# Four banks for an up-projection, two loads taken by turns, and a convolution that is not paused, in a hybrid encoder layer

## The chip, the cores and the metric

The kernel runs on one NeuronCore of a Trainium2 chip. The metric is the device time of one execution in microseconds (us); a time for a kernel is the median of its runs. A profile is one more execution, recorded by the hardware profiler, and its times count from the first instruction of its span. The engines are PE (TensorE, matmuls; PEld is its weight loads), DVE (VectorE), ACT (ScalarE), POOL (GpSimd) and SP (SyncE, which issues most DMAs).

## What is computed

One encoder layer, run on two requests that share all weights: a prompt of 512 rows and a sample of 1024 rows, 1024 wide, all in fp32.

```python
def _trunk(x, ...):                       # called for the prompt and for the sample
    h = _rmsnorm(x, norm_attn_g)
    z = h @ w_in                          # 1024 x 1792: q, k, v, ca, cb
    a_out = _window_attn(q, k, v, ...)    # 8 heads, 2 kv heads, |q-k| <= 128, bias, sink
    c = ca * sigmoid(cb)
    c = _dwconv(c, conv_dw_w, conv_dw_b)  # 31 taps, 512 channels
    c = silu(_layernorm(c, ...))
    x = x + concat([a_out, c]) @ w_out
    h = _rmsnorm(x, norm_ffn_g)
    u = _dwconv(h @ w_up, ffn_dw_w, ffn_dw_b)            # 3 taps, 5632 channels
    x = x + (silu(u[..., :2816]) * u[..., 2816:]) @ w_down
    return _rmsnorm(x, norm_final_g)
```

## The kernel before, in words

**Numbers.** Every fp32 matmul operand is split into two fp32r parts, `hi` (a cast on ACT) and `lo` (a subtraction on POOL or DVE). A product is three matmuls per 128 rows of contraction: hi·hi, hi·lo, lo·hi. A weight block of 128 columns is split by `split` (L158): one ACT instruction (L161) and one POOL instruction (L162).

**Tiling.** Activations are held transposed, 128 channels on the partitions by 512 tokens: one piece for the prompt (`nt` 0), two for the sample (`nt` 1 and 2). A product of a weight block with one piece (`proj`, L304) is 8 x 3 = 24 matmuls of 128x512 into one PSUM bank.

**Banks.** Up to the sample's MLP the eight PSUM banks have names: three `a`, two `u`, two `b`, one `c`. The table `use` (L123, updated at L853, L902, L1005, L1026, L1052) says which letters a job may take, and `Slots.tile` (L82) takes the first free one in the order in which they were given back. In the prompt's MLP the jobs are: `up` (the products), `gate` (on `b`), `attn` and `turn` (on `a`), `norm` (on `a` and `u`, then `a`), `conv` (on `c`).

**Start.** SP issues the loads in program order. First come the prompt's transposed input in eight chunks and the first weight block in five pieces. Then `load_rows(0)` (L209) loads the prompt's four blocks of 128 rows, 512 KB each, and `load_xT(1)` (L199) the sample's first piece, transposed, in four chunks of 512 KB. The rows feed `row_scale(0)` (L492): a sum of squares of each block (ACT L247 and DVE L249 by turns), a reciprocal root on POOL (L145, L146), four ACT spreads (L255), four PE transposes (L258) and an ACT copy (L499); the result scales the products of the prompt when they are taken from their banks (`evac`, L388). The transposed chunks feed `raw_h1` (L471): one ACT (L474) and one DVE instruction (L475) per 128 channels. `beside` (L515) makes the products of the first two weight blocks with one piece: 48 matmuls at L519, for the prompt, then the sample's pieces.

**Middle.** The prompt's projection, convolution (`conv_items`) and attention run beside the projection of the sample; then the prompt's output projection. The sample's convolution (`late_items`, L366) is a queue `late` of steps: one DVE instruction per tap (L345), every second one with a tap on ACT and POOL (L336, L337) while there are some left to hand over.

**The prompt's MLP.** Twenty-two pieces (L1044). `ffn_step(k)` (L996) makes two products, gate half and value half, with weights that were split a piece earlier. `up_half` (L942) takes a product from its bank with one ACT (L958) and two DVE instructions (L954), the last readers of the bank; `gate` (L972) puts the halves together in a `b` bank (ACT L974, DVE L975 and L976) and stores the result. Beside it run the sample's attention (`side`) and `late`. Both are advanced by `tick` (L286), which `proj` calls three times and `up_mm` once per product: each call adds `pace["late"]` to a credit, and queue steps are issued while there is credit; a tap costs 0.13 + 512/960 = 0.663 of it. `pace["late"]` is `CD` = 0.65 from piece `LK` on and 0 before.

**Then** come the sample's output projection and its MLP on wide banks, a seven-product (Strassen-like) scheme, up-projection and down-projection.

**Order.** The program text gives priorities. A planner orders each engine's instructions by a simulated timeline and these priorities, so an engine may run a later piece of text first when the earlier one isn't ready in the simulation. On the chip each engine keeps the planned order. From L1345 on the order of PE is that of the text.

Of the kernel before, what the change touches and what calls it, by code (L numbers as in the profile page):

```python
# [59 lines left out]
SA, N2, SA2 = 4, 99, 4  # L60
KL, WN = 16, 7
LN = 3
LK = 1
AHEAD = (1, 1, 1, 2, 2)
XQ, H2, LATE2 = (1, 5), 2, (4,)
SUM_AT = (4, 6, 8, 10, 12, 14, 16, 18)
# [41 lines left out]
def tile_hybrid_encoder(ctx: ExitStack, tc: tile.TileContext, xs, rel_bias, norm_attn_g, w_in,  # L108
# [11 lines left out]
    sb = Slots(lambda tag: sml if tag[0] == "s" else big,  # L120
               dict(q=(15, 4096), c=(4, 4352), h=(61, 2048), d=(2, 2304), s=(33, 64)))
    banks = Slots(lambda tag: ps[two_of[tag]], dict(a=(3, 2048), u=(2, 2048), b=(2, 2048), c=(1, 2048)))
    use = dict(step="aub", turn="aub", conv="c", attn="au", norm="b", out="b", up="u", down="b")  # L123

    def sm(n):
        return sb.tile([n])
# [1 line left out]
    def bank(job):  # L128
        return banks.tile([NT], among=use[job])
# [18 lines left out]
    def load_x(G, tt):  # L148
        x = sb.tile([D])
        nc.sync.dma_start(x[:], G["x"][tt * P:(tt + 1) * P, :])  # L150
        return x
# [23 lines left out]
    def want_raw(i):  # L175
        if i < nch and i not in raws and i not in ws:
            raws[i] = chunk_raw(laid["w_in"], order[i][2] // P)

    def want_w(i):
        if i < nch and i not in ws:  # L180
            want_raw(i)
            ws[i] = split(raws.pop(i))
# [16 lines left out]
    def load_xT(nt):  # L199
        n = 1 if nt == 0 else 2  # L200
        for k in range(0, KC, n):
            x = sb.tile([n, NT])
            nc.sync.dma_start(x[:], xT[nt][k:k + n].rearrange("k p t -> p k t"))
            for m in range(n):
                xq[nt, k + m] = (x, m)
            x = None
            yield

    def load_rows(nt):  # L209
        G, t0 = (GR[0], 0) if nt == 0 else (GR[1], 4 * (nt - 1))  # L210
        for tt in range(4):
            xq[nt, "row", tt] = load_x(G, t0 + tt)

    def drawn(items):
        for _ in items:
            pass
# [12 lines left out]
    for i, n in enumerate(AHEAD):  # L229
        load_first(i, nc.sync)  # L230
        for _ in range(n):
            next(x_of_prompt)
    drawn(x_of_prompt)
    load_rows(0)
    drawn(load_xT(1))
    for _ in range(NW // 4):
        pt = bank("step")
        for i in range(4):
# [232 lines left out]
    def raw_h1(nt, kc):  # L471
        t, m = xq.pop((nt, kc))
        x, hi, lo = t[:, m, :], sb.tile([NT], F32R), sb.tile([NT], F32R)
        nc.scalar.activation(hi[:], x, AF.Identity, scale=gA[:, kc:kc + 1])  # L474
        nc.vector.scalar_tensor_tensor(lo[:], x, gA[:, kc:kc + 1], hi[:].bitcast(F32), op0=ALU.mult, op1=ALU.subtract)  # L475
        h1.setdefault(nt, []).append((hi, lo))
# [15 lines left out]
    def row_scale(nt):  # L492
        ss, rs = sm(4), sm(4)
        for tt in range(4):
            square_sum(xq.pop((nt, "row", tt)), ss[:, tt:tt + 1], tt)
        rstd_of(ss[:], D, rs[:])
        pt = spread(rs, "turn")
        rbs[nt] = sb.tile([NT])
        nc.scalar.copy(rbs[nt][:], pt[:])  # L499
# [7 lines left out]
    def landed(i, nt, pp):  # L507
        kind, c, col = order[i]
        evac(kind, c, nt, pp[:])
        if kind == "ca" and nt != 1:  # L510
            g = min(nt, 1)
            (convs, late)[g].append((conv_items, late_items)[g](c, cpads.pop((g, c))))
        tick()

    def beside(nt, kc, first=False):  # L515
        hi, lo = h1[nt][kc]
        for L, R in ((0, hi), (0, lo), (1, hi)):
            for c in range(2):
                nc.tensor.matmul(pps[nt, c][:], ws[c][L][:, kc, :], R[:], start=(kc == 0 and L == 0 and R is hi),  # L519
                                 stop=(kc == KC - 1 and L == 1))  # L520
# [16 lines left out]
    ends = cvw[:, :(CK - 1) * 4].rearrange("p (s h c) -> p h s c", h=2, c=4)  # L537
    nc.gpsimd.tensor_tensor(csum[:, :CK // 2 * 4].rearrange("p (s c) -> p s c", c=4), ends[:, 0], ends[:, 1], op=ALU.add)
    nc.gpsimd.tensor_copy(csum[:, CK // 2 * 4:CK // 2 * 4 + 4], cvw[:, (CK - 1) * 4:CK * 4])
    load_rows(1)  # L540
    for kc in range(KC):
        raw_h1(1, kc)

    def constants():
        nc.vector.tensor_scalar_mul(vecs[:, 20:28], vecs[:, 20:28], 0.5)
        nc.vector.tensor_scalar_mul(vecs[:, 50:72], vecs[:, 50:72], 0.5)
        halves = fw[:, :132].rearrange("p (t f) -> p t f", t=3)[:, :, 22:44]
        nc.vector.tensor_scalar_mul(halves, halves, 0.5)
        nc.vector.tensor_scalar_mul(nsink[:], sinkb[:], -1.0)
# [28 lines left out]
    for nt in range(3):  # L578
        if nt:
            pps.update({(nt, c): bank("step") for c in range(2)})  # L580
            for kc in range(KC):
                beside(nt, kc)
        if nt == 1:
            for kc in range(KC):
                raw_h1(2, kc)
            want_w(2)
            row_scale(1)
            want_raw(3)
            load_rows(2)
            constants()  # L590
        if nt == 2:
            row_scale(2)
            want_w(3)
        for i in range(2):
            landed(i, nt, pps.pop((nt, i)))
# [238 lines left out]
    def double_keys():  # L834
        for kv in range(NKV):
            for L in range(2):
                nc.gpsimd.tensor_copy(kt[1, kv][L][HD:P, :], kt[1, kv][L][0:HD, :].bitcast(F32))
                yield
# [28 lines left out]
    def prompt_out():  # L867
        for n in range(2):
            for kc in range(KC):
                if (kc, n) not in wor:  # L870
                    load_wo(kc, n)
            yield 0.0
            for kc in range(KC):
                split_wo(kc, n, kc % 2 < DW)
                if kc % 2 == 1:
                    yield 0.0
            for i in range(4):
                if n == 0 and i == 3:
                    for kc in range(WOP):
                        load_wo(kc, 1)  # L880
                while i not in ready:
                    yield 0.0
                yield from out_half(i, n)
            wo.clear()
        bias.clear()
        load_bias(1)
        yield from make_h2(0, 0)
# [19 lines left out]
    out = deque([prompt_out()])  # L907
    n, doubling = 0, double_keys()
# [135 lines left out]
    for k in range(NJ):  # L1044
        at[0] = k
        if k == LK:
            pace.update(late=CD)
# [34 lines left out]
    A, rows = {}, {}  # L1082
# [631 lines left out]
    u, e, o11, o12 = (acc.pop(n) for n in ("u", "e", "o11", "o12"))  # L1714
# [108 lines left out]
```

## Time and profile before

| | |
|---|---|
| time, median of 3 runs | 1501.19 us (1499.17 to 1506.18) |
| the profiled execution | 1498.89 us |
| its span, first to last instruction | 1497.1 us |
| PE, DVE, ACT, POOL busy | 1473.5, 1119.2, 803.7, 770.7 us |
| mean DMA rate | 152 GB/s |
| mean granted TensorE clock | 0.999 |

A busy time is the union of an engine's instructions. Matmuls overlap: a row gives 389 ns for one, and 112 of them run in 25 us. Idle time of PE is therefore read from the gaps, not from the rows' sums. A wait is put down to the instruction whose semaphore came last; that name can be of a neighbour that ended at the same moment.

### The profile page before, as it was taken

Reading aid. Unit: us, or ns where it says so; the run is one execution under the profiler, and the core shown is the slowest. Engines: PE = TensorE matmul, PEld = TensorE weight load, DVE = VectorE, ACT = ScalarE, POOL = GpSimd, SP = SyncE. Lnnn points to the kernel's source line nnn. Section 1 sums busy time; section 2 is a strip of 40 time slices with the busy share of each in tenths; the row PEclk is TensorE's granted clock in tenths of the full one; section 3 lists DMA queues with packets and bytes.
Section 4 is the critical chain, followed back from the end, with each engine's and each line's share of the span. In section 5 each row is a group of like instructions: output and inputs, shape, how many; then the busy total and the mean of one; then the engine's idle time right before and its main releaser. Section 6 shows DMA issues by size and latency. Waiting matters only on the chain.

```text
span 1497.1 us, 19881 instructions
## 1 busy us (share of the span) xinstructions
PE 1473.5 (98%) x6736; PEld 1211.2 (81%) x6736; DVE 1119.2 (75%) x1512; ACT 803.7 (54%) x1421; POOL 770.7 (51%) x687
## 2 busy tenths in 40 slices
PE   9999999999999999999999999999999999999998
PEld 7888778877888888878878888888888888888886
DVE  7877935649898998575768888888887856578774
ACT  7424455567777676653465544544454543343355
POOL 3455353347878776432336666565555242135546
PEclk9999999999999999999999999999999999999999
DMA  9554241743344454663214333334342495356644
GB/s 368 187 153 144 91 113 36 242 159 127 127 139 136 130 166 141 209 216 116 79 57 137 131 125 129 125 121 129 132 134 68 155 315 187 116 194 213 222 167 162
DMA packets 124626, 228.19 MB, mean 152 GB/s; under 512 B 20420, under 2 KB 45764, under 8 KB 124397
## 3 DMA queue, kind: packets, MB, share of 16 engines
q1 hardware_dynamic: 124092, 226.37, 46.1%
q8 instruction: 53, 0.87, 0.3%
q10 hardware_dynamic: 432, 0.56, 0.1%
q14 instruction: 49, 0.39, 0.1%
HBM read 166.83 MB, written 61.10 MB: 152 GB/s over the span
## 4 chain that ended last, share of the span: by engine, by line
PE 74%; DVE 5%; DMA 3%; POOL 3%; issue 2%; ACT 2%; SPq 0%; POOLq 0%; DVEq 0%; ACTq 0%
PE w L1187 8%; PE w L1189 8%; PE w L1188 8%; PE w L1519 7%; PE w L1520 7%; PE w L1521 7%; PE u L308 5%; PE u L309 5%; PE u L310 5%; PE b L310 2%; PE b L308 2%; PE b L309 2%; PE a L685 1%; PE a L643 1%; DVE c L345 1%
## 5 line engine op out<-in xcount | busy, mean ns | idle before, releaser
L162 POOL TENSOR_TENSOR q<-q,q 128x1024 fp32r<-128x1024 f32 x66 | 158.8, 2407 | 77.2 <-ACT q L161 51.1
L1067 POOL TENSOR_TENSOR q<-q,q 128x512 fp32r<-128x512 f32 x81 | 116.5, 1447 | 126.7 <-ACT q L1173 126.7
L1067 DVE TENSOR_TENSOR h<-h,h 128x512 fp32r<-128x512 f32 (+1 forms) x152 | 129.5, 881 | 55.4 <-ACT h L1075 21.8
L1521 PE MATMUL w<-h,h 128*128 128x512 f32 x432 | 168.1, 389 | 0.0
L1519 PE MATMUL w<-h,h 128*128 128x512 f32 x432 | 168.1, 389 | 0.0
L1520 PE MATMUL w<-h,h 128*128 128x512 f32 x412 | 160.3, 389 | 0.0
L308 PE MATMUL u<-h,q 128*128 128x512 f32 x384 | 150.8, 393 | 2.5 <-DVE s L658 2.1
L310 PE MATMUL u<-h,q 128*128 128x512 f32 x384 | 150.6, 392 | 0.0
L309 PE MATMUL u<-h,q 128*128 128x512 f32 x384 | 150.3, 391 | 0.0
L1187 PE MATMUL w<-h,q 128*128 128x512 f32 x368 | 143.8, 391 | 0.5 <-ACT w L1260 0.4
L1189 PE MATMUL w<-h,q 128*128 128x512 f32 x368 | 143.7, 391 | 0.0
L1188 PE MATMUL w<-h,q 128*128 128x512 f32 x347 | 135.5, 390 | 0.0
L1067 POOL TENSOR_TENSOR h<-h,h 128x512 fp32r<-128x512 f32 (+1 forms) x38 | 51.8, 1364 | 142.8 <-ACT h L1502 123.9
L1075 ACT CAST h<-h 128x512 fp32r<-128x512 f32 x116 | 69.2, 620 | 103.4 <-DVE h L1067 27.9
L161 ACT CAST q<-q 128x1024 fp32r<-128x1024 f32 x66 | 69.2, 1049 | 53.9 <-PE u L309 24.0
L345 DVE SCALAR_TENSOR_TENSOR c<-d,cvw,c 128x512 f32<-128x512 f32 x128 | 95.9, 749 | 1.5
L337 POOL TENSOR_TENSOR h<-h,h 128x512 f32<-128x512 f32 x62 | 80.8, 1304 | 28.8 <-ACT h L336 26.9
L1521 PEld LDWEIGHTS w<-h,h 128*128 128x128 f32 x432 | 81.1, 188 | 16.9
L1519 PEld LDWEIGHTS w<-h,h 128*128 128x128 f32 x432 | 81.1, 188 | 16.9
L1067 POOL TENSOR_TENSOR c<-q,c 128x512 fp32r<-128x512 f32 x46 | 72.0, 1572 | 42.0 <-ACT c L1173 42.0
L1520 PEld LDWEIGHTS w<-h,h 128*128 128x128 f32 x412 | 77.3, 188 | 15.9
L308 PEld LDWEIGHTS u<-h,q 128*128 128x128 f32 x384 | 72.1, 188 | 16.9 <-ACT h L336 2.3
(474 smaller groups left out, 4019.4 us busy)
## 6 DMA issues: line engine op xcount, KB each, us to landing
q<-in_laid_w_up SPq DMA_DIRECT2D x88, 512.0 KB, 3.9
ga<-q SPq DMA_DIRECT2D x65, 256.0 KB, 2.2
h<-gap SPq DMA_DIRECT2D x57, 256.0 KB, 3.5
h<-ga SPq DMA_DIRECT2D x57, 256.0 KB, 3.4
h<-in_w_down SPq DMA_DIRECT2D x52, 256.0 KB, 3.5
q<-in_laid_w_in SPq DMA_DIRECT2D x22, 512.0 KB, 4.1
gap<-h SPq DMA_DIRECT2D x44, 256.0 KB, 3.1
q<-in_x_sample SPq DMA_DIRECT2D x15, 512.0 KB, 7.2
```

What stands on the lines that cost most here:

```text
L162: (nc.vector if dve else nc.gpsimd).tensor_tensor(lo[:], raw[:], hi[:].bitcast(F32), op=ALU.subtract)
L308: nc.tensor.matmul(out, whi[:, kc, :], hi[:], start=(kc == 0), stop=False)
L309: nc.tensor.matmul(out, whi[:, kc, :], lo[:], start=False, stop=False)
L310: nc.tensor.matmul(out, wlo[:, kc, :], hi[:], start=False, stop=(kc == KC - 1))
L345: nc.vector.scalar_tensor_tensor(acc[:], src(t), w(t), acc[:], op0=ALU.mult, op1=ALU.add)
L1067: (eng or nc.vector).tensor_tensor(out, a, b, op=ALU.subtract)
L1187: nc.tensor.matmul(out, whi[:, s], hi[:], start=(start and c == 0), stop=False, **go)
L1188: nc.tensor.matmul(out, whi[:, s], lo[:], start=False, stop=False, **go)
L1189: nc.tensor.matmul(out, wlo[:, s], hi[:], start=False, stop=(stop and c == 3), **go)
L1519: nc.tensor.matmul(out, sh[:, c], th[:], start=(p == 0 and not seeded), stop=False, **go)
L1520: nc.tensor.matmul(out, sh[:, c], tl[:], start=False, stop=False, **go)
L1521: nc.tensor.matmul(out, sl[:, c], th[:], start=False, stop=(p == NPAIR - 1), **go)
```

## The change

`use["up"]` becomes `"ub"`: the products of the prompt's MLP may take the two `u` banks and the two `b` banks, which `gate` also takes. `LK` becomes 0: `late` goes on through piece 0. `load_rows` becomes a generator; at the start SP issues by turns one block of rows and one chunk of the sample's transposed input. The other two calls of `load_rows` draw all four blocks at once, as before.

```diff
-LK = 1
+ROWS = (1, 1, 1, 1)
+LK = 0
...
-    use = dict(step="aub", turn="aub", conv="c", attn="au", norm="b", out="b", up="u", down="b")
+    use = dict(step="aub", turn="aub", conv="c", attn="au", norm="b", out="b", up="ub", down="b")
...
         for tt in range(4):
             xq[nt, "row", tt] = load_x(G, t0 + tt)
+            yield
...
-    load_rows(0)
-    drawn(load_xT(1))
+    rows, x_of_sample = load_rows(0), load_xT(1)
+    for n in ROWS:
+        for _ in range(n):
+            next(rows)
+        next(x_of_sample)
+    drawn(rows)
+    drawn(x_of_sample)
...
-    load_rows(1)
+    drawn(load_rows(1))
...
-            load_rows(2)
+            drawn(load_rows(2))
```

## The prediction

> **What bounds the kernel now.** I read the page's busy times first, then PE's time in stretches that follow the stages, then PE's waits, and then the order of time at the two places that these point to.
>
> ```profile
> span 1497.1 us, 19881 instructions
> PE 1473.5 (98%) x6736; PEld 1211.2 (81%) x6736; DVE 1119.2 (75%) x1512; ACT 803.7 (54%) x1421; POOL 770.7 (51%) x687
> ...
> PE 74%; DVE 5%; DMA 3%; POOL 3%; issue 2%; ACT 2%; SPq 0%; POOLq 0%; DVEq 0%; ACTq 0%
> ```
>
> PE works 1473.5 of 1497.1 us: it stands still for 23.6 us in all. The change issues the same matmuls, so it can only move these 23.6 us. The next view has PE alone by stretches (length, PE busy, instructions, clock, DMA).
>
> ```profile
> core 0: us, PE busy (x), PEclk, DMA share, GB/s
> 0.00:25.00 25.00, 21.53 (x89) 1.00 0.95 345
> 25.00:150.00 125.00, 125.00 (x566) 1.00 0.58 186
> 150.00:338.00 188.00, 181.80 (x883) 1.00 0.42 127
> 338.00:364.00 26.00, 22.75 (x104) 1.00 0.39 134
> 364.00:636.00 272.00, 271.56 (x1294) 1.00 0.47 149
> 1300.00:1325.00 25.00, 25.00 (x112) 1.00 0.49 151
> ```
>
> Idle: 3.5 us in the first 25, none to 150, 6.2 to 338, 3.3 in the first pieces of the prompt's MLP, 0.4 in the rest of it. The last row gives the pace: 25 / 112 = 0.223 us per matmul where all are 128x512; I take 0.23 in the busier early stages. The waits name what ended the idle times (waiter, releaser: us in total, times, longest):
>
> ```profile
> PE u L308 <- DVE s L658: 2.1, 1, 2.1
> PE a L519 <- ACT h L474: 1.8, 1, 1.8
> PE b L308 <- DVE h L457: 1.3, 1, 1.3
> PE a L643 <- DVE s L647: 1.1, 1, 1.1
> PE a L685 <- DVE s L647: 1.0, 2, 0.5
> PE u L308 <- DVE h L954: 0.4, 1, 0.4
> ```
>
> The two longest are the places of the change. No wait comes back piece after piece.
>
> **Rows by turns.** The start, in order of time (start, length, engine, line; [idle before it <- what ended it]):
>
> ```profile
> 13.69 1.06 ACT L247 ACTIVATE h<-q 128x1024 bf16<-128x1024 f32 x1 [0.51 <-DMA q<-in_x_prompt]
> 16.22 1.06 ACT L247 ACTIVATE h<-q 128x1024 bf16<-128x1024 f32 x1 [1.38 <-DMA q<-in_x_prompt]
> 17.36 0.39 PE L519 MATMUL b<-h,h 128*128 128x512 f32 x1
> 17.44 1.23 DVE L249 CUSTOM_DVE_ANT_0 h<-q 128x1024 bf16<-128x1024 f32 x1 [1.21 <-DMA q<-in_x_prompt]
> 18.73 1.34 ACT L474 ACTIVATE h<-q,vecs 128x512 fp32r<-128x512 f32 x2 [1.35 <-DMA q<-in_laid_xsT]
> 19.50 2.45 PE L519 MATMUL a<-h,h 128*128 128x512 f32 x8 [1.75 <-ACT h L474]
> 21.79 0.38 PE L258 MATMUL b<-ident,h 128*128 128x128 f32 x2
> 25.05 0.56 ACT L499 COPY h<-b 128x512 f32<-128x512 f32 x1
> 26.29 0.68 DVE L395 TENSOR_TENSOR h<-u,h 128x512 f32<-128x512 f32 x1
> 42.22 0.39 PE L308 MATMUL b<-h,q 128*128 128x512 f32 x1
> ```
>
> ACT and DVE were waiting for each transfer, so these starts are its landings: the first block of rows at 13.7, the third at 16.2, the fourth at 17.4, the sample's first chunk at 18.7. A 512 KB transfer lands every 1.25 us. The prompt's last matmul starts at 17.36, PE could go on at 17.59, and it begins the sample's at 19.50: 1.91 us lost, for the chunk that is fifth in the row. By turns the chunk is second and lands near 13.7 + 1.25 = 14.95. ACT has ended its sum of squares at 14.75, so the first `hi` is there at 15.7 and its `lo`, at 0.75 us, near 16.5: PE does not wait. Two 128-channel steps of `beside` need 12 x 0.23 = 2.7 us and a chunk now comes every 2.5; the fourth lands at 22.5 as before and is wanted at 17.6 + 3 x 2.7 = 25.7, with 1.5 us for ACT and DVE. So -1.9 us. The price: the fourth block of rows lands at about 21.2, 3.8 us later, and so do the sums, POOL's root, L258 (21.8 to 25.6), L499 (28.9) and the first L395 (30.1). Who needs them: the banks that L395 frees, first asked for after the products that start at 42.2; 12 us of cover. The SP queue holds the same eight issues, so nothing behind them moves. Is the 1.9 kept? From 25 to 150 PE never waits, so it is carried to 150. At 154 to 158 PE waits for DVE (1.1 and 1.3 us above) with DVE nearly full:
>
> ```profile
> 125.00:150.00 25.00, 25.00 (x123) 20.92 (x122) 23.27 (x48) 11.95 (x30) 13.27 (x16) 1.00 0.44 130
> 77.68 0.70 DVE L409 TENSOR_TENSOR u<-u,h 128x512 f32<-128x512 f32 x1 [5.37 <-PE u L310]
> ```
>
> DVE had 5.4 us of idle behind PE at 77.7, so DVE's own work moves up with PE there. I take -1.9; bounds -2.0 and +3.8 (L258's delay, if PE has to wait for it in its order).
>
> **Four banks.** The first pieces of the prompt's MLP:
>
> ```profile
> 343.72 2.42 POOL L162 TENSOR_TENSOR q<-q,q 128x1024 fp32r<-128x1024 f32 x1
> 345.04 3.92 DVE L345 SCALAR_TENSOR_TENSOR c<-c,csum,c 128x512 f32<-128x512 f32 x5
> 348.85 2.42 POOL L162 TENSOR_TENSOR q<-q,q 128x1024 fp32r<-128x1024 f32 x1
> 351.19 1.45 ACT L958 ACTIVATE h<-u,vecs,fw 128x512 f32<-128x512 f32 x2
> 352.98 0.74 DVE L954 SCALAR_TENSOR_TENSOR h<-u,fw,h 128x511 f32<-128x511 f32 x1
> 353.12 0.66 PE L685 MATMUL a<-ident,h 128*128 128x128 f32 x4 [0.54 <-DVE s L647]
> 354.30 1.40 DVE L954 SCALAR_TENSOR_TENSOR h<-u,fw,h 128x511 f32<-128x511 f32 x2
> 355.84 0.47 PE L308 MATMUL u<-h,q 128*128 128x512 f32 x1 [2.07 <-DVE s L658]
> ```
>
> PE has ended the transposes of 353.12 at 353.78 and the third product starts at 355.84. It needs the bank of the first, whose taps are L954 at 352.98 and the second of the pair at 354.30, ended at 355.70; the named L658 is a reciprocal that it does not read. Its weights were split by 346.1 (L162 at 343.72). Before the MLP eight transposes go over `u`, `u`, `c`, `b`, `b`, so the free order is u, u, b, b: the third product now takes a `b` bank, free since the transposes. That takes away 2.07 us, and the 0.4 us of the other product that waits for L954: -2.5. What is late next: the fourth product takes the first's bank, at 353.78 + 24 x 0.23 = 359.3; the taps end at 355.7 and its weights at 351.3 (L162 at 348.85): covered. The 0.5 us waits at L685 are on `a` banks and stay. Bounds: -2.8 (start to start instead of idle) and 0 (the wait goes over to the next product).
>
> **Gates on the same banks.** By the free order every third piece from piece 4 on begins with a product on a bank that a gate two pieces back gave up; six times.
>
> ```profile
> 386.91 0.69 DVE L976 TENSOR_TENSOR h<-b,h 128x512 f32<-128x512 f32 x1
> 393.62 0.47 PE L308 MATMUL u<-h,q 128*128 128x512 f32 x1
> ```
>
> Piece 2's gate ends at 387.6 and piece 4's first product starts at 393.6: 6.0 us of cover, so 0.
>
> **Convolution not paused.** Piece 0 gets 8 ticks x 0.65 = 5.2 of credit, 5.2 / 0.663 = 8 taps: on DVE 8 x 0.749 = 6.0 us, and 4 taps handed over, on POOL 4 x 1.304 = 5.2 us.
>
> ```profile
> L345 DVE SCALAR_TENSOR_TENSOR c<-d,cvw,c 128x512 f32<-128x512 f32 x128 | 95.9, 749 | 1.5
> L337 POOL TENSOR_TENSOR h<-h,h 128x512 f32<-128x512 f32 x62 | 80.8, 1304 | 28.8 <-ACT h L336 26.9
> ```
>
> The planner had already put taps there (five at 345.04), so part of the 8 is no new work in piece 0. In POOL's queue they stand before the splits for the fourth product, done 8.0 us ahead of need: covered. On DVE they stand before the first product's taps: at worst 355.7 + 6.0 = 361.7 against 359.3, +2.4 us. Best -1.0, if the two L685 waits go with the new order. I take 0, as DVE's own idle and the taps already there are nearest.
>
> **Sum.** 1498.9 - 1.9 - 2.5 = 1494.5 for a profiled execution. That one lay 2.3 below the median of the runs, so 1496.8: 1497.
>
> **Rivals.** *Given back*: DVE, not PE, paces 150 to 175 and the first pieces (the 23.27 of 25 above), so PE comes earlier and waits longer. Against it is DVE's idle at 77.7. It gives 1500 to 1501. [...] The trace shows the bank as the cause of the one, so I give this a quarter.
>
> *The row scale stalls PE (slower)*: L258 stood behind 8 matmuls of the sample. If the plan leaves it so, PE reaches it at 17.6 + 8 x 0.23 = 19.4 and waits to 25.6; PE is 3.8 late instead of 1.9 early: 1501.2 + 3.8 - 2.5 = 1502.5. It decides when L258 stands before the 35th of the 48 matmuls ((25.6 - 17.6) / 0.23). Against it: the planner knows the new loads. [...]
>
> *Gates hold the banks (slower still)*: if gates end over 6.0 us later, six products wait. With gates 8 us later it is 6 x 2 = 12: 1509. It needs a DVE order that no row shows.
>
> *More than the sum*: the new plan also closes half of the 6.2 us between 150 and 338 and the two L685 waits: 1497 - 4 = 1493.
>
> **Chances.** Forecast 0.52, given back 0.25, row scale 0.08, gates 0.05, more 0.10. Range: 1491 takes in the lower bounds (-2.0, -2.8, -1.0) and most of the last case; 1504 the row scale; only gates and tails are left out. This kernel's measurement tells 0.5%, 7.5 us, from no change: under 1493.7 lies part of the last case and scatter, 0.09; over 1508.7 the gates, 0.05; the rest, 0.86, between.
>
> **What would show it.** Right: no wait of L519 for L474 near 17 to 20, and the sample's products begin by 17.8; no wait of an up product for L954 or L658; PE's idle sum near 19 us. Wrong: L258 after an idle PE; products that wait for L976; L345 ahead of L954 with PE idle at 359; or the waits near 155 grown by 1.9.

## The result, and the profile after

The changed kernel takes 1497.95 us (median of 17 runs, 1496.36 to 1501.16), the kernel before 1501.75 in the 17 runs beside them (1499.01 to 1506.18). The ratio is 0.9974, 95% interval 0.9967 to 0.9982: 2.7 to 5.0 us faster, inside the 0.5% that I called no change. The forecast was 1497.0 with the range 1491 to 1504. The sum behind it did not come out so well, and that the two times lie so near each other is luck: two gains were put too small, one term was nought and is a loss, and a fourth effect was not in the sum.

The page of the changed kernel, its busy times and the shares of the chain:

```profile
span 1496.9 us, 19874 instructions
PE 1475.7 (99%) x6736; PEld 1215.0 (81%) x6736; DVE 1120.4 (75%) x1512; ACT 801.8 (54%) x1421; POOL 771.9 (52%) x687
...
PE 87%; DVE 4%; DMA 3%; POOL 3%; ACT 2%; issue 1%; SPq 0%; POOLq 0%; DVEq 0%; ACTq 0%
```

The profiled span is 0.2 us shorter than before's 1497.1, though the medians are 3.8 apart. PE's idle time fell from 23.6 to 1496.9 - 1475.7 = 21.2, that is -2.4; but PE's busy time rose from 1473.5 to 1475.7, +2.2, with the same 6736 matmuls. They ran slower. The same stretches as in the prediction (length, PE busy, instructions, clock, DMA), and one more:

```profile
core 0: us, PE busy (x), PEclk, DMA share, GB/s
0.00:25.00 25.00, 23.22 (x96) 1.00 0.95 346
25.00:150.00 125.00, 124.33 (x565) 1.00 0.59 190
150.00:338.00 188.00, 179.59 (x858) 0.98 0.40 122
338.00:364.00 26.00, 25.92 (x119) 0.95 0.43 142
364.00:636.00 272.00, 272.00 (x1299) 1.00 0.47 151
...
150.00:165.00 15.00, 12.51 (x50) 0.77 0.20 69
```

Length less busy gives the idle time of each, against before: 1.8 (3.5), 0.7 (0), 8.4 (6.2), 0.1 (3.3), 0 (0.4). The start and the prompt's MLP gained 1.7 + 3.2 + 0.4 = 5.3 us; the stretch in between gave back 0.7 + 2.2 = 2.9. And the clock column, 1.00 in all these rows of before, reads 0.98 and 0.95 here, and 0.77 from 150 to 165. PE's waits (waiter, releaser: us in total, times, longest; code lines of this kernel stand 7 higher than before in the parts below, so L519 is L526, L308 is L315, L954 is L961):

```profile
PE a L650 <- DVE h L716: 2.7, 1, 2.7
PE a L246 <- POOL ident masks.py:199: 1.5, 1, 1.5
PE c L274 <- DVE q L854: 1.5, 1, 1.5
PE b L315 <- DVE h L464: 1.3, 1, 1.3
PE a L706 <- ACT h L694: 1.2, 1, 1.2
...
PE a L650 <- DVE s L654: 1.1, 1, 1.1
...
PE a L315 <- ACT h L506: 0.7, 1, 0.7
```

The wait of L519 for the sample's chunk and all up-products' waits for L658 and L954 are gone. New are the first and the third row, 2.7 and 1.5 us, the fifth, 1.2 us near the end of the prompt's MLP, and the last.

### The profile page after: what moved, and what is told of

It is laid out like the page before. It is cut to its first block, busy times and chain, and to the rows that moved or that the text cites. A ratio compares the mean times of both kernels' runs of the same rounds, so it can differ in the third digit from the quotient of the medians.

```text
span 1496.9 us, 19874 instructions
## 1 busy us (share of the span) xinstructions
PE 1475.7 (99%) x6736; PEld 1215.0 (81%) x6736; DVE 1120.4 (75%) x1512; ACT 801.8 (54%) x1421; POOL 771.9 (52%) x687
## 4 chain that ended last, share of the span: by engine, by line
PE 87%; DVE 4%; DMA 3%; POOL 3%; ACT 2%; issue 1%; SPq 0%; POOLq 0%; DVEq 0%; ACTq 0%
PE w L1194 8%; PE w L1196 8%; PE w L1195 8%; PE w L1527 7%; PE w L1526 7%; PE w L1528 7%; PE b L315 5%; PE b L317 4%; PE b L316 4%; PE u L315 4%; PE u L316 4%; PE u L317 4%; PE a L650 1%; PE a L692 1%; PE u L796 1%
## 5 line engine op out<-in xcount | busy, mean ns | idle before, releaser
L1194 PE MATMUL w<-h,q 128*128 128x512 f32 x368 | 143.9, 391 | 0.8 <-ACT w L1285 0.4
L315 PE MATMUL b<-h,q 128*128 128x512 f32 x312 | 124.8, 400 | 1.9 <-DVE h L464 1.3
L316 PE MATMUL b<-h,q 128*128 128x512 f32 x312 | 123.4, 396 | 0.0
L317 PE MATMUL b<-h,q 128*128 128x512 f32 x312 | 123.3, 396 | 0.0
L317 PE MATMUL u<-h,q 128*128 128x512 f32 x272 | 106.6, 393 | 0.0
L315 PE MATMUL u<-h,q 128*128 128x512 f32 x272 | 106.5, 392 | 0.0
L316 PE MATMUL u<-h,q 128*128 128x512 f32 x272 | 106.4, 392 | 0.0
L352 DVE SCALAR_TENSOR_TENSOR c<-d,cvw,c 128x512 f32<-128x512 f32 x128 | 96.0, 750 | 1.6
L1526 PEld LDWEIGHTS w<-h,h 128*128 128x128 f32 x432 | 81.1, 188 | 17.0
L1528 PEld LDWEIGHTS w<-h,h 128*128 128x128 f32 x432 | 81.1, 188 | 16.9
L344 POOL TENSOR_TENSOR h<-h,h 128x512 f32<-128x512 f32 x62 | 81.0, 1308 | 26.1 <-ACT h L343 21.7
```

The source lines that it names most:

```text
L315: nc.tensor.matmul(out, whi[:, kc, :], hi[:], start=(kc == 0), stop=False)
L316: nc.tensor.matmul(out, whi[:, kc, :], lo[:], start=False, stop=False)
L317: nc.tensor.matmul(out, wlo[:, kc, :], hi[:], start=False, stop=(kc == KC - 1))
L352: nc.vector.scalar_tensor_tensor(acc[:], src(t), w(t), acc[:], op0=ALU.mult, op1=ALU.add)
L1194: nc.tensor.matmul(out, whi[:, s], hi[:], start=(start and c == 0), stop=False, **go)
L1526: nc.tensor.matmul(out, sh[:, c], th[:], start=(p == 0 and not seeded), stop=False, **go)
```

## The experiments

Twelve kernels, five rounds each, every one against the kernel before that ran beside it on the same chip. The first three split the change.

| kernel | turns | banks | convolution runs from piece | median us | ratio | 95% interval |
|---|---|---|---|---|---|---|
| changed kernel | yes | 4 | 0 | 1497.95 | 0.9974 | 0.9967 to 0.9982 |
| e1_rows | yes | 2 | 1 | 1500.13 | 0.9982 | 0.9972 to 0.9991 |
| e2_banks | no | 4 | 1 | 1498.42 | 0.9971 | 0.9959 to 0.9983 |
| e3_conv | no | 2 | 0 | 1502.12 | 0.9998 | 0.9988 to 1.0008 |
| e4_rows_banks | yes | 4 | 1 | 1495.7 | 0.9954 | 0.9942 to 0.9965 |
| e5_paused_two | yes | 4 | 2 | 1491.91 | 0.9930 | 0.9916 to 0.9943 |
| e6_half_rate | yes | 4 | 0, half rate | 1498.44 | 0.9970 | 0.9957 to 0.9983 |
| e7_chunks_first | chunks first | 4 | 1 | 1499.49 | 0.9979 | 0.9970 to 0.9987 |
| e8_b_alone | yes | 2, with the gates | 1 | 1571.51 | 1.0460 | 1.0443 to 1.0476 |
| e9_paused_three | yes | 4 | 3 | 1499.31 | 0.9978 | 0.9969 to 0.9986 |
| e10_paused_five | yes | 4 | 5 | 1500.47 | 0.9991 | 0.9980 to 1.0002 |
| e11_pause_alone | no | 2 | 2 | 1505.68 | 1.0022 | 1.0012 to 1.0032 |
| e12_no_handover | yes | 4 | 0, no hand-over in the first list | 1495.44 | 0.9960 | 0.9947 to 0.9974 |

**e1_rows, e2_banks, e3_conv: one part alone.** The edits are the parts of the diff above: the turns; `up="ub"`; `LK = 0`.

> Only the turns of the two loads; up-products on two banks, convolution paused in piece 0. My theory (each part works at its own place, the parts add): the wait at 17 to 20 us is gone (-1.9), up to 0.7 comes back near 46 us where a product waits for a bank that the later row scale holds, and the bank wait of 2.1 us near 354 is still there: 1 to 2 us under the kernel before, ratio 0.9990. Rival (the planner's new order decides, not the parts): the start is better but new waits stand elsewhere before the prompt's MLP, as the changed kernel has them at 332 to 338 us (2.7 and 1.5): no gain, ratio 1.000 or above.

> Only the four banks. My theory: PE's order is that of before up to the third product, which moves ahead of the attention's score and transpose matmuls; idle time from 338 to 636 us falls from 3.7 to under 0.5: 3 us under the kernel before, ratio 0.998. Rival (the bank wait goes over to a later wait, such as a gate on the same bank or the first product's taps): idle time in that stretch stays at 2 us or more, ratio 0.9995 to 1.000.

> Only the convolution not paused in piece 0. My theory as forecast: nothing, ratio 0.999 to 1.001. New theory after the changed kernel's trace: the taps, raised in priority, stand ahead on DVE just before the MLP and bring the waits of 2.7 and 1.5 us at 332 to 338: 2 to 4 us over the kernel before, ratio 1.002, and idle time from 150 to 338 rises from 6.2 to 8 or more. Rival: these waits belong to the rows by turns, and this kernel has none of them.

By the ratios times 1502, the turns bring 2.7 us, the banks 4.4, the convolution 0.3 with an interval over both signs. Their sum would be 7.4; the whole change brought 3.9. So the parts do not seem to add up, as if one of them cost something only beside the others.

Two signs came out otherwise than the texts above have them. In e2 the up-products' waits are gone, but idle time from 338 to 636 us falls only from 3.7 to 2.5: a wait of 2.2 us in the attention (L699 for ACT's L687) now lies between 600 and 636. Taken from 338 to 700, over the end of the MLP, idle falls from 5.9 to 3.1, in the changed kernel to 2.4. In e3 idle from 150 to 338 rises only to 7.0, and the waits foreseen as 2.7 and 1.5 are 0.8 and 1.2.

**e4_rows_banks: the change without its third part.**

```diff
-LK = 0
+LK = 1
```

> Rows by turns and four banks, convolution paused in piece 0 as before. If the waits at 332 to 338 are the convolution's: none of them here, and it is 5 us under the kernel before and 1 to 2 under the changed kernel, ratio 0.9965. If they come from the rows by turns or from the planner's new order: they are here too, ratio 0.9975 like the changed kernel. If the convolution had brought the gain: ratio 0.999.

0.9954 is what e1 and e2 add up to (0.9982 x 0.9971 = 0.9953). Its interval lies below the changed kernel's: with the other two parts in place, the unpaused convolution costs 0.0020 x 1502 = 3 us, of the 7 that they bring.

**Where the convolution costs: order of time at the end of the middle stage.** First the changed kernel, then e4 (start, length, engine, line; idle before it and what ended it). L344 is a convolution tap on POOL, L147 POOL's root for a row scale, L854 the scaling that the transposes L274 read, L716 what the scores L650 wait for.

```profile
334.09 1.27 POOL L344 TENSOR_TENSOR h<-h,h 128x512 f32<-128x512 f32 x1
334.71 0.68 DVE L716 TENSOR_TENSOR h<-a,h 64x512 f32<-64x512 f32 x1 [1.74 <-ACT h L715]
335.45 0.54 POOL L147 TENSOR_TENSOR rs<-rs,nhalf 128x1 f32<-128x1 f32 x1
335.54 0.59 PE L650 MATMUL a<-q,h 128*128 128x384 f32 x2 [2.66 <-DVE h L716]
335.96 1.26 POOL L344 TENSOR_TENSOR h<-h,h 128x512 f32<-128x512 f32 x1
336.02 1.76 DVE L854 TENSOR_SCALAR q<-q,rs 128x1024 f32<-128x1024 f32 x1 [0.63 <-POOL rs L147]
337.84 0.48 PE L274 MATMUL c<-ident,q 128*128 128x128 f32 x1 [1.47 <-DVE q L854]
```

```profile
329.92 0.55 POOL L147 TENSOR_TENSOR rs<-rs,nhalf 128x1 f32<-128x1 f32 x1
330.50 0.76 DVE L854 TENSOR_SCALAR q<-q,rs 128x1024 f32<-128x1024 f32 x1 [0.52 <-POOL rs L147]
331.31 0.33 PE L274 MATMUL c<-ident,q 128*128 128x128 f32 x1 [0.62 <-DVE q L854]
331.70 0.68 DVE L716 TENSOR_TENSOR h<-a,h 64x512 f32<-64x512 f32 x1
```

L147 runs 5.5 us later and L716 3.0 us later. Of that, 2.3 us are there before this stretch begins (the same four scores L650 start at 318.65 and at 316.38): in this execution the clock reads 0.50 from 156.2 to 163.1 us, and in that of e4 1.00 from 150 to 338. The rest, 3.2 and 0.7 us, is new here, and L854 takes 1.76 us instead of 0.76, beside a tap on POOL. Credit in piece 0 made the planner put taps before the MLP begins. On which engine? POOL's groups from 320 to 338 in the changed kernel, then in e4:

```profile
L344 POOL TENSOR_TENSOR h<-h,h 128x512 f32<-128x512 f32 x4 | 5.1, 1270 | 0.1
```

```profile
L344 POOL TENSOR_TENSOR h<-h,h 128x512 f32<-128x512 f32 x1 | 1.3, 1292 | 0.0
```

DVE has no tap of L352 that starts in these 18 us in either kernel. The theory was therefore: not the taps on DVE, which the prediction had priced, but those handed over to ACT and POOL. Two kernels test it.

**e6_half_rate: half the credit in piece 0.** If the number of taps in piece 0 decides, half of them should cost half.

```diff
         if k == LK:
+            pace.update(late=CD / 2)
+        if k == 1:
             pace.update(late=CD)
```

> The changed kernel with the convolution at half its rate in piece 0 only (0.325 instead of 0.65 per tick). Theory (taps ahead of the row scales): fewer taps get a place before the MLP, so the two waits of 2.7 and 1.5 us at 332 to 338 are halved or gone: ratio 0.996 to 0.997, between the kernel with a pause and the changed one. Rival (it is on or off: the planner pulls as many taps forward as soon as the queue is open): the same waits, ratio 0.9975.

0.9970 (0.9957 to 0.9983): at the theory's upper end and close to the rival's 0.9975; the interval takes in both. POOL again has four taps of L344 from 320 to 338, but the two waits are shorter:

```profile
PE a L650 <- DVE h L716: 1.6, 1, 1.6
PE c L274 <- DVE q L854: 1.2, 1, 1.2
```

That is 2.8 us together, against 4.2 in the changed kernel and 1.1 in e4; idle from 150 to 338 is 7.4, against 8.4 and 5.9. So half the credit puts as many taps ahead, as the rival has it, but halves what the waits have more than in e4, as the theory has it. The time shows little of that gain. In this execution the clock reads 0.98 from 150 to 338 us, 0.94 from 338 to 364 and 0.94 from 600 to 660; in the changed kernel it is 0.98, 0.95 and 1.00.

**e12_no_handover: convolution in piece 0, but nothing handed over.** Code lines behind the edit stand 3 higher.

```diff
-        nc.vector.tensor_tensor(pacc[:], acc[:], pacc[:], op=ALU.add)
+        if noff:
+            nc.vector.tensor_tensor(pacc[:], acc[:], pacc[:], op=ALU.add)
+        else:
+            nc.vector.tensor_copy(pacc[:], acc[:])
...
-        both = yield from taps(late, odd, ..., ns, LOFF[0], with_bias(c))
+        both = yield from taps(late, odd, ..., ns, LOFF[0] if c else 0, with_bias(c))
```

> The changed kernel (convolution running through piece 0), but the six taps of the first list of the first channel that ACT and POOL take over (L343, L344) are done by DVE instead, so no such tap stands in ACT's and POOL's queues ahead of the MLP; DVE gets six more taps (6 x 0.75 = 4.5 us). Theory (the cost of the unpaused convolution is its taps on ACT and POOL between 320 and 338 us, which put off POOL's root L147 and the copies L714 and L715 and slow DVE's scaling L854): the waits for L716 (2.7) and for L854 (1.5) are gone or under 0.8 each, L147 ends near 330.5 as in the kernel with turns and four banks alone, PE's idle from 150 to 338 is 5.0 to 6.2 us, and the ratio is 0.9940 to 0.9962 against 0.9974. Rival (it is the taps on DVE itself, ahead of L716 and L854): both waits stay or grow, idle from 150 to 338 is 8 or more, and the ratio is 0.9970 to 0.9990.

0.9960 (0.9947 to 0.9974), beside e4's 0.9954. The root and the scaling are where e4 has them, and idle from 150 to 338 is 188 - 182.48 = 5.5 us:

```profile
330.35 0.55 POOL L147 TENSOR_TENSOR rs<-rs,nhalf 128x1 f32<-128x1 f32 x1
330.94 0.75 DVE L857 TENSOR_SCALAR q<-q,rs 128x1024 f32<-128x1024 f32 x1 [0.26 <-POOL rs L147]
...
150.00:338.00 188.00, 182.48 (x883) 0.99 0.42 127
```

The wait for L716 is gone and 0.4 us is left of that for L854, although DVE has six taps more. So the hand-over to ACT and POOL causes these two waits; the rival, DVE's taps, falls. The time agrees with it but does not settle it alone: the interval still overlaps the changed kernel's.

**e5_paused_two, e9_paused_three, e10_paused_five: a longer pause.** If taps before and in the first pieces are in the way, a longer pause than before's should bring more.

```diff
-LK = 0
+LK = 2
```

(3 and 5 in the other two.)

> Rows by turns, four banks, the sample's convolution paused through the first two pieces. Theory (the convolution's taps on ACT and POOL are planned ahead of the last row scales of the prompt's output, at 325 to 337 us, when the text gives them a place in piece 0): pausing longer takes more of them away, idle time from 150 to 338 us stays at 6 or falls to 5, no wait over 1 us at 328 to 338; ratio 0.995 to 0.9965, and 5 to 6 us of DVE work come later, where the last pieces may wait. Rival (any other plan scatters by 2 us): 0.9975 with a wait somewhere new.

> Rows by turns, four banks, convolution paused through pieces 0 to 2. Theory (what a pause does is keep the convolution's ACT and POOL taps away from the row scales ahead of the MLP): two pieces have taken all but one of these taps from 320 to 338 us, so a third wins nothing there; the convolution ends one piece, some 13 us, later, which the remaining 19 pieces have room for: ratio 0.9925 to 0.9935, as with two. Rival (DVE is less full in the first pieces and that is the gain): a further 2 us, ratio 0.9915.

> The same, paused through pieces 0 to 4. Theory: the taps that are put off (5 x 5.2 of credit, 40 taps, 30 us of DVE) fill the last pieces; with DVE at 48 of 50 us in the busiest stretch the sample's convolution ends later than its attention, and the sample's first output rows wait for it: idle time from 600 to 660 us rises by 2 to 10 us, ratio 0.995 to 1.000. Rival (there is room to the end): 0.993.

A pause of two pieces gives 0.9930 (0.9916 to 0.9943), 1491.91 us: faster than both kernels, the fastest of all, and more than its text foresaw; its interval just touches e4's. Idle from 150 to 338 is 5.1 us, and POOL has no tap from 320 to 338. Three is a miss, 0.9978; five gives 0.9991, as expected. What the pause takes away comes back at the end of the MLP, where the sample's attention and output projection want the convolution done. The stretch from 600 to 660 in the kernels with a pause of two, three and five:

```profile
600.00:660.00 60.00, 56.36 (x273) 1.00 0.66 219
```

```profile
600.00:660.00 60.00, 55.05 (x245) 0.91 0.65 211
```

```profile
600.00:660.00 60.00, 52.28 (x237) 0.94 0.65 212
```

Idle is 3.6, 5.0 and 7.7 us, and in the last two the clock falls. From two to three pieces the profiled span grows by 9.3 us (1489.3 to 1498.6), the idle here by only 1.3. In all, PE's idle sum grows by 2.2 (17.7 to 19.9), and 13.7 us at half clock are new (the clock reads 0.91 from 600 to 660 and 0.99 from 150 to 338, with two pieces 1.00 in both). By the two paces in the last section they cost at most 13.7 x 0.47 = 6.4 us, an estimate: 2.2 + 6.4 = 8.6 of the 9.3. The part from 150 to 338 stands ahead of the pause, where another execution may not have it. Why the clock falls with the third piece of pause was not tried.

**e11_pause_alone: is it the pause itself?** Before, with `LK = 2` and nothing else.

> The kernel before with the convolution paused through two pieces instead of one; two up banks, rows first. Theory: the taps are gone from 320 to 338 us here too, and the bank wait of 2.1 us near 354 stays or shrinks, as the first product's taps no longer stand behind five convolution taps on DVE: ratio 0.997 to 0.9985. Rival (it works only with the four banks): 0.9995 to 1.0005.

1.0022: slower, another miss. With two banks its page names

```profile
PE u L308 <- DVE h L954: 3.2, 3, 1.9
```

so the up-products still wait for their two banks, and PE is idle for 5.5 us from 600 to 660 (2.2 in before). So the pause does not pay by itself. This kernel lacks the turns of the loads as well as the four banks; that it is the banks that the pause needs is argued from these waits, not tried apart.

**e7_chunks_first: the price of late rows.**

```diff
-ROWS = (1, 1, 1, 1)
-LK = 0
+ROWS = (0, 0, 0, 0)
+LK = 1
```

> Four banks, pause as before, and at the start all four chunks of the sample's input ahead of the four blocks of rows. Tells how much cover the row scale has: the first block of rows lands at 18.7 instead of 13.7 us, the last at 22.5, 1.3 us later than by turns. Theory (cover of 12 us on the banks): the start is as by turns, no wait of L526 for L481 near 17; ratio as with the turns, 0.9955. Rival (the row scale's transposes stall PE): PE idles 2 us or more before them at 25 to 28 us; ratio 0.997.

0.9979 against e4's 0.9954: 3.8 us lost. PE's waits name the row scale, and PE's rows from 49 to 53 the clock:

```profile
PE a L265 <- ACT h L262: 2.1, 1, 2.1
...
49.00:53.00 4.00, 3.44 (x9) 0.51 0.00 0
```

The transposes L265 that wait here are those of the second row scale. That is like the rival "the row scale stalls PE", but at 46 to 48 us rather than 19, and at another row scale than the one it named. One row block and one chunk by turns pay 0.7 at the same place (the last row of the changed kernel's waits).

**e8_b_alone: what do the four banks hide?** The products and the gate on the same two `b` banks.

```diff
-LK = 0
+LK = 1
...
-    use = dict(..., up="ub", down="b")
+    use = dict(..., up="b", down="b")
```

> Rows by turns, pause as before, the up-products on the two b banks alone, which the gates take too: two banks for three users a piece. Tests the cover of gates. If a gate's bank has some 6 us of cover only because four banks go round, each piece now waits for its gate: 22 pieces x 2 to 6 us, 40 to 130 us over the kernel before, ratio 1.03 to 1.09. If the gates are early enough anyway (rival), it is like two u banks: a few waits of 2 us, ratio 0.998 to 1.002.

1.0460, 69 us over the kernel before. Against e4, the profiled span is 79.7 us longer; PE idles 62.3 us instead of 20.5, and 58 us run at half clock (it reads 0.87 from 338 to 364 and 0.92 from 364 to 636), by the paces in the last section at most 58 x 0.47 = 27 us: 42 + 27 = 69 of the 79.7. Little of that is named as an up-product's wait for its bank (the last row):

```profile
PE a L706 <- ACT h L694: 16.0, 11, 2.8
PE a L692 <- DVE s L654: 12.5, 11, 3.4
...
PE b L315 <- DVE h L961: 3.9, 5, 1.4
```

The loss is named in the sample's attention, which is woven between the products. That it comes bunched where products have no bank to go to is my reading of these names, not tested. What is shown is that products and gates on two banks cost 69 us, where the gates cost nothing with the `u` banks beside them.

## Why the prediction was right or wrong

**Rows by turns, -1.9: right in place, the cover not whole.** The sample's products follow the prompt's without a gap:

```profile
17.59 0.39 PE L526 MATMUL b<-h,h 128*128 128x512 f32 x1
17.81 2.43 PE L526 MATMUL a<-h,h 128*128 128x512 f32 x10
```

The first 25 us gained 1.7. The "12 us of cover" held for the first row scale. But a product at 46.8 waits 0.67 us for L506, a copy of the second row scale's stage: its transposes start at 45.5 as before (45.6), while PE's products come earlier. I followed the first row scale to its reader and not the second. e1 gave -2.7 us (0.9972 to 0.9991: 1.4 to 4.2). The waits at 154 to 158, 1.08 and 1.34 us, are the same in both kernels: nothing was given back there.

**Four banks, -2.5: right mechanism, too small.** The first matmul of the third product, and the first tap that it would have waited for:

```profile
354.25 0.39 PE L315 MATMUL b<-h,q 128*128 128x512 f32 x1
355.07 0.75 DVE L961 SCALAR_TENSOR_TENSOR h<-u,fw,h 128x511 f32<-128x511 f32 x1 [1.15 <-ACT h L965]
```

The third product takes a `b` bank, as the free order said, and starts right behind the product on `u`; PE idles 0.1 us from 338 to 364 instead of 3.3, and not at all to 636. That is 3.2 + 0.4 = 3.6, and by idle from 338 to 700 it is the same (5.9 to 2.4; in e2, the banks alone, 2.8). The term was too small by the waits that were to stay ("the 0.5 us waits at L685 are on `a` banks and stay"): the planner, with a bank free, sets the product ahead of the attention's score and transposes, and those waits have cover. e2 gave -4.4 us (0.9959 to 0.9983: 2.6 to 6.2).

The wait of 2.1 us for a bank came once, not piece after piece, and it was the bank all the same: in e2, where only the banks are more, it is gone.

**Gates, 0: right.** No product waits for L976 (L983) in the profile after. e8 shows what stands behind that.

**Convolution, 0, bounds -1.0 to +2.4: wrong, +3.** The step that failed is "in POOL's queue they stand before the splits for the fourth product ... covered". The taps handed over were priced against POOL's later work in the MLP; the planner put them earlier, ahead of L147, L714 and L715 of the stage before. I had written that the planner "had already put taps there (five at 345.04)", and did not ask what else stands in ACT's and POOL's queues 15 us ahead. From 320 to 338 one tap stands in POOL's queue in e4, four in the changed kernel. Taken alone (e3) the part puts five there, but it moved idle time and kept its sum: 0.8 us more from 150 to 338, less in the MLP, 23.9 in all against 23.6. Why it costs more beside the other two parts stays open.

**The clock, not in the sum.** The rows of before in the prediction read a clock of 1.00, and they are of one execution. Each run has its mean granted clock. Over the 80 runs of the kernel before beside the experiments it was 0.994 in four (mean 1506.1 us), 0.996 in 24 (1502.5) and 0.999 in two (1499.2). The profiled execution, 2.3 below the median and at 0.999 as well, was one with hardly any slow stretch. Over all 196 runs of these kernels and of before, e8 left out, each set against its own kernel's mean, 0.001 of clock goes with 1.1 us (correlation -0.74). Mean clocks: before 0.9963, e2 0.9973, e4 and e5 0.9982, changed kernel 0.9951. The changed kernel has 0.0031 less clock than e4, by that slope 3.4 us; PE's idle sums in the two profiles differ by only 0.7 (21.2 and 20.5), since e4 waits 1.4 longer at one place near 824 us, in the sample's MLP (L1194 for ACT's L1285). That is 4.1 together, against a loss of 3 us that the intervals leave between 0.3 and 6.0. How it divides into waits and clock stays open: the slope is drawn from the runs as they came, and no kernel set the clock by itself. The two also lie side by side in the traces. In the changed kernel's profile the clock reads 0.50 from 156.2 to 163.1 us, beginning in the second of the waits at 154 to 158, which e4 has as well (1.1 and 1.3 us) at 1.00; and from 337.2 to 340.6, beginning in the second of the two new waits of 2.7 and 1.5 us, where e4 reads 1.00. That a part of what the clock takes belongs to the convolution is my reading of this, not shown.

**The sum.** 1.9 + 2.5 = 4.4 was forecast, 3.9 came: 2.7 + 4.4 by e1 and e2, less 3. That these nearly cancel is luck; PE's idle sum, forecast near 19 us, is 21.2. The upper end of the range, 1504, lies 1.5 above the 1502.5 of the "row scale" rival; no run shows the term that this stands for. What the runs showed at a row scale is PE's wait of 2.1 us and a clock of 0.51 from 49 to 53 us in e7, which takes 1499.49 us. "More than the sum", 0.10, had half the mechanism (the L685 waits close; the 6.2 us from 150 to 338 do not, 5.9 in e4). Without the third part the time would have come out between it and the forecast: e4, 1495.7. "Given back", 0.25, did not happen where it was looked for. The "gates" rival did not show, the "row scale" one only in e7.

## What to carry to other kernels

Where a planner fills engines from a queue, opening the queue earlier moves work to every engine that the queue feeds, and to before the place where the credit is given: look at the queues of the helpers (here ACT and POOL) over the stretch ahead, not at the engine that does most of it. Try the parts of a change one at a time and in pairs: the fastest kernel here (0.9930) came from turning the third part round beside the other two. And compare profiles by idle time and clock apart, since executions of one kernel differ by several us at different mean clocks (the kernel before: 1506.1 us at 0.994, 1499.2 at 0.999).

## What the runs showed of the hardware

**The same waits, with and without a lower clock.** In the changed kernel's profile the granted clock reads 0.50 in two stretches, 156.2 to 163.1 us and 337.2 to 340.6 us, and 1.00 in all others up to 1488 us; in the profile of before it reads 1.00 throughout up to 1488. The waits at 154 to 158, 1.08 and 1.34 us, stand in both. Over the 14 profiles the clock from 150 to 338 us reads under 1.00 in 8. What decides between the two was not shown. The waits are in both rows below, before and the changed kernel, with 12.51 us busy in each, and 62 matmuls against 50:

```profile
150.00:165.00 15.00, 12.51 (x62) 1.00 0.27 99
```

```profile
150.00:165.00 15.00, 12.51 (x50) 0.77 0.20 69
```

At a clock of 0.50 the matmuls of 512 columns start every 0.427 us (changed kernel, twelve steps from 157.63 to 162.75), at 1.00 every 0.227 (before, four from 158.97 to 159.88). So a stretch of 6.8 us at 0.50 costs at most 6.8 x (1 - 0.227/0.427) = 6.8 x 0.47 = 3.2 us, an estimate from these two paces.

**DVE beside POOL.** L854 takes 0.75 us without a tap beside it and 1.76 when a tap L344 runs on POOL: it starts at 336.02, the tap ends at 337.22, it ends at 337.78. In the changed kernel it runs four times: 1.77 and 1.76 us where a tap begins 0.06 us ahead of it (328.07 and 335.96), 0.75 in the other two, where no tap runs beside it. In the two slow places it ends 0.54 and 0.56 us after the tap. In before and in e4 all four take 0.75 to 0.76; in e3, without the pause, two of the four take 1.90 and 1.75. Why it is slower there was not shown; no run tries it apart.
